# A delta-rule chain that closes its groups two at a time: stages in alternation, the output scale as one GpSimd product, the gates loaded into the product's tile

## The chip, the cores and the metric

The kernel runs on one core of one Trainium2 chip. The metric is the device time of one execution in microseconds (us), start to end; three runs of the kernel before are known. Beside them there is one execution taken by the hardware profiler, with a record for each instruction and each transfer. The five engines are called by their short names in the rows: PE is TensorE (matmuls and transposes), PEld its weight loads, DVE is VectorE, ACT is ScalarE, POOL is GpSimd, and SP is SyncE, which here only issues DMAs. Each engine goes through its own instructions in order.

## The reference

One layer of a bidirectional encoder on 2048 tokens of width 1024. Its branch A is a gated delta rule with 8 heads of width 128, run forward and backward over the sequence and summed; branch B is a long convolution. This is the part that matters:

```
def step(S, xs):
    q_i, k_i, u_i, w_i, attn_i, gl_i = xs
    v_new = u_i - jnp.einsum("nhcd,nhde->nhce", w_i, S)
    o = jnp.einsum("nhcd,nhde->nhce", q_i, S) + jnp.einsum("nhij,nhje->nhie", attn_i, v_new)
    S = S * gl_i[..., None, None] + jnp.einsum("nhcd,nhce->nhde", k_i, v_new)
    return S, o
```

The outputs of both directions are added; per head and token the sum is divided by the root of its mean square, multiplied by a SiLU gate (and by a weight), and projected back to width 1024.

## The kernel before

The stages follow each other: norms, projections, the inner inverses of the delta rule for each chunk, then the chain (method `chain`), then the output projection of branch A (`dn_out`, L1303) and what is left of branch B. The sequence is cut into 16 chunks of 128 tokens for each of the 8 heads, and the chain has 128 steps n; head h = n // 16, step in the head s = n % 16. In step s the forward direction (d = 0) handles chunk s and the backward direction (d = 1) chunk 15 - s, with a state S of 128x128 each. A step is a chain of dependent work between TensorE and the engines that empty its results: `ch <- S, kvq` (L1202), R on VectorE (L1203), `ch <- R, ep` (L1211), Y (L1214 on ScalarE for d = 1, L1216 on VectorE for d = 0), `ch <- Y, kt` (L1223), the new S (L1226) and the outputs o (`po`, L1208 and L1231, emptied at L1238 to L1242). Between them the method yields, and matmuls of an independent projection (`pj`, L635) fill TensorE.

From s = 8 on each step completes two chunks of outputs, since both directions have then been there. Four chunks that lie side by side are a group `o` of 128x4x128, with the sums of squares in `msq` (L1245). After s = 11 and after s = 15 two groups are complete, so there are 16 pairs, 32 groups in all. `finish` closes a group:

- it loads four columns of the norm (`sc <- sqd`, 128x4, 2 KB), and works out the scale with two small operations of VectorE (L1163, L1164) and a power on GpSimd (L1165);
- it loads the gate (`z <- sz`, 128x512, 256 KB);
- it scales o by `sc`, one column for each of four blocks (L1170, four ScalarE activates);
- it transposes the four blocks on TensorE into a PSUM tile (L1174, one buffer) and multiplies them with the gate on VectorE (L1176), then stores the product `og`.

`both` runs `finish` for the first group of a pair and then for the second; the loop over n calls `next(fin)` once at the end of each step, so that a stage of closing goes into a step.

TensorE's instructions keep the order in which the code issues them. The order of the other engines is set ahead of time by a scheduler that sorts instructions by the time at which it expects them to be ready, so that work written for a later step can stand in an earlier place. All loads and stores go through SyncE's one queue (L178 load, L181 store). A tile with k buffers is used in turn: the load of the k-th next one has to wait until the reader of this one is done. Names in the rows: `kvq` and `ep` are the operands of a step (loaded two steps ahead, kvq scaled on GpSimd, L1146), `kt` and `tk` the turned k of the next step (`turn`), `wraw`, `oraw` and `rf` loaded weights and rows which other engines split in two parts (`hh`, `hl`, L206 and L209), `gt`, `th` the gates of branch B.

Of the kernel before, what the change touches and what calls it, by code (L numbers as in the profile page):

```python
# [11 lines left out]
F32 = mybir.dt.float32  # L12
F32R = mybir.dt.float32r
AF = mybir.ActivationFunctionType
ALU = mybir.AluOpType
# [141 lines left out]
class Ring:  # L157
# [6 lines left out]
    def next(self):  # L164
        t = self.t[self.i % len(self.t)]
        self.i += 1
        return t


class K:  # L170
# [949 lines left out]
    def chain(self, P, pp, kvq, ep, sqd, sz_dram, og_dram):  # L1120

        nc = self.nc
        N = H * NCH
        for n in ("eg", "gt", "es"):
            setattr(self, n, P.tile([128, NCH, 16], F32, name=n))
        self.kn = P.tile([128, H, NCH], F32, name="kn")
        nc.gpsimd.memset(self.kn, 0.5)
        nc.gpsimd.tensor_tensor(self.kn, self.ss, self.kn, op=ALU.pow)
        g = self.g
        for d in range(2):  # L1130
            ds_ = slice(8 * d, 8 * d + 8)
            for m, o in ((self.mi[d], self.eg), (self.msr[:, d], self.es), (self.ones, self.gt)):
                ps = pp.tile([128, NCH, 8], F32, name="cs", tag="tr")
                nc.tensor.matmul(ps, lhsT=m, rhs=g[:, :, ds_], start=True, stop=True)
                nc.scalar.activation(o[:, :, ds_], ps, AF.Exp)
        ops, kts = {}, {}
        at = lambda n, d: (n // NCH, n % NCH if d == 0 else NCH - 1 - n % NCH)

        def fetch(n):
            for d in range(2):  # L1140
                h, c = at(n, d)
                a = P.tile([128, 3, 128], F32, name=f"kvq{d}", bufs=3)
                self.load(a, kvq[h][c])
                b = P.tile([128, 2, 128], F32, name=f"ep{d}", bufs=3)
                self.load(b, ep[h][d, c])
                nc.gpsimd.tensor_scalar(a[:, 1], a[:, 1], self.kn[:, h, c:c + 1], None, op0=ALU.mult)  # L1146
                ops[n, d] = (a[:, 0], a[:, 1], a[:, 2], b[:, 0], b[:, 1])

        def turn(n):
            ps = pp.tile([128, 2, 128], F32, name="tk", tag="tr")  # L1150
            for d in range(2):
                nc.tensor.transpose(ps[:, d], ops[n, d][0], self.ident)
            for d in range(2):
                h, c = at(n, d)
                kts[n, d] = P.tile([128, 128], F32, name=f"kt{d}", bufs=2)
                nc.scalar.activation(kts[n, d], ps[:, d], AF.Copy, scale=self.es[:, c, 8 * d + h:8 * d + h + 1])

        def finish(h, g, o, msq):

            cs = slice(4 * g, 4 * g + 4)  # L1160
            sc = P.tile([128, 4], F32, name="sc", bufs=2)
            self.load(sc, sqd[h, 512 * g:512 * g + 512].rearrange("(c p) -> p c", p=128))
            nc.vector.tensor_scalar(sc, sc, EPS, 128.0 * EPS, op0=ALU.add, op1=ALU.mult)  # L1163
            nc.vector.scalar_tensor_tensor(sc, msq, 1.0 / 128.0, sc, op0=ALU.mult, op1=ALU.add)  # L1164
            nc.gpsimd.tensor_tensor(sc, sc, self.mhalf[:, :4], op=ALU.pow)  # L1165
            z = P.tile([128, 512], F32, name="z")
            self.load(z, sz_dram[h, :, 512 * g:512 * g + 512])
            yield
            for j in range(4):
                nc.scalar.activation(o[:, j], o[:, j], AF.Copy, scale=sc[:, j:j + 1])  # L1170
            yield
            ps = pp.tile([128, 4, 128], F32, name="tr", tag="tr")
            for j in range(4):
                nc.tensor.transpose(ps[:, j], o[:, j], self.ident)  # L1174
            og = P.tile([128, 512], F32, name="og")
            nc.vector.tensor_tensor(og, ps.rearrange("p a b -> p (a b)"), z, op=ALU.mult)  # L1176
            self.store(og_dram[h, :, 512 * g:512 * g + 512], og)
            yield

        fin = iter(())  # L1180
        fetch(0)
        fetch(1)
        turn(0)
        for n in range(N):
            h, s = n // NCH, n % NCH
            if s == 0:
                St, O, M = [None, None], {}, {}
            if n + 2 < N:
                fetch(n + 2)
            info = []  # L1190
            for d in range(2):
                c = at(n, d)[1]
                ci = slice(8 * d + h, 8 * d + h + 1)
                k, vr, q, e, p = ops.pop((n, d))
                ps = pp.tile([128, 3, 128], F32, name=f"ch{d}")
                po = pp.tile([128, 2, 128], F32, name="po", bufs=3)
                info.append((c, ci, k, vr, q, e, p, ps, po))
            R, Y = [None, None], [None, None]
            for d, (c, ci, k, vr, q, e, p, ps, po) in enumerate(info):
                R[d] = P.tile([128, 128], F32, name=f"R{d}")  # L1200
                if s:
                    nc.tensor.matmul(ps[:, 0], lhsT=k, rhs=St[d], start=True, stop=True)  # L1202
                    nc.vector.scalar_tensor_tensor(R[d], ps[:, 0], self.eg[:, c, ci], vr, op0=ALU.mult, op1=ALU.subtract)  # L1203
                else:
                    nc.vector.tensor_scalar(R[d], vr, -1.0, None, op0=ALU.mult)
            for d, (c, ci, k, vr, q, e, p, ps, po) in enumerate(info):
                if s:
                    nc.tensor.matmul(po[:, 0], lhsT=q, rhs=St[d], start=True, stop=True)  # L1208
            yield
            for d, (c, ci, k, vr, q, e, p, ps, po) in enumerate(info):  # L1210
                nc.tensor.matmul(ps[:, 1], lhsT=e, rhs=R[d], start=True, stop=True)  # L1211
                Y[d] = P.tile([128, 128], F32, name=f"Y{d}", bufs=2)
                if d:
                    nc.scalar.activation(Y[d], ps[:, 1], AF.Copy, scale=self.an[:, c, ci])  # L1214
                else:
                    nc.vector.tensor_scalar(Y[d], ps[:, 1], self.an[:, c, ci], None, op0=ALU.mult)  # L1216
            if n + 1 < N:
                turn(n + 1)
            yield
            for d, (c, ci, k, vr, q, e, p, ps, po) in enumerate(info):  # L1220
                kt = kts.pop((n, d))
                if s < NCH - 1:
                    nc.tensor.matmul(ps[:, 2], lhsT=kt, rhs=Y[d], start=True, stop=True)  # L1223
                    Sn = P.tile([128, 128], F32, name=f"S{d}", bufs=2)
                    if s:
                        nc.vector.scalar_tensor_tensor(Sn, St[d], self.gt[:, c, ci], ps[:, 2], op0=ALU.mult, op1=ALU.add)  # L1226
                    else:
                        nc.vector.tensor_copy(Sn, ps[:, 2])
                    St[d] = Sn
            for d, (c, ci, k, vr, q, e, p, ps, po) in enumerate(info):  # L1230
                nc.tensor.matmul(po[:, 1], lhsT=p, rhs=Y[d], start=True, stop=True)  # L1231
                g, j = c // 4, c % 4
                if g not in O:
                    O[g] = P.tile([128, 4, 128], F32, name="o", bufs=6)
                    M[g] = P.tile([128, 4], F32, name="msq", bufs=6)
                o = O[g][:, j]
                if s < 8:
                    nc.scalar.activation(o, po[:, 1], AF.Copy)  # L1238
                else:
                    nc.vector.tensor_tensor(o, po[:, 1], o, op=ALU.add)  # L1240
                if s:
                    nc.vector.scalar_tensor_tensor(o, po[:, 0], self.eg[:, c, ci], o, op0=ALU.mult, op1=ALU.add)  # L1242
                if s >= 8:
                    jk = P.tile([128, 128], F32, name="jk")
                    nc.scalar.activation(jk, o, AF.Square, accum_out=M[g][:, j:j + 1])  # L1245
            if s >= 8 and s % 4 == 3:
                for _ in fin:
                    pass

                def both(h, gs, O, M):  # L1250
                    for g in gs:
                        yield from finish(h, g, O[g], M[g])

                fin = both(h, (s // 4, 3 - s // 4), dict(O), dict(M))
            next(fin, None)
            yield
        for _ in fin:
            pass
# [258 lines left out]
```

## Time and profile before

| what | us |
|---|---|
| three runs, median | 3554.59 |
| three runs, lowest and highest | 3553.59, 3556.47 |
| the profiled execution's own time | 3549.07 |
| its span, first to last instruction | 3547.0 |
| TensorE busy in the span | 3319.6 (94%) |
| VectorE, ScalarE, GpSimd busy | 2088.7 (59%), 1489.7 (42%), 1431.3 (40%) |
| the chain, 2288 to 2866 of the span: length, TensorE busy | 578.00, 536.17 |

The profiled execution lies 5.5 us below the median of the runs, and 2.1 us of it lie outside of the span. Sums of rows are to be set against the profiled execution; times of a changed kernel against the runs. In the rows, a number in brackets is the idle time of the engine ahead of the instruction, with the instruction or transfer that ended it.

### The profile page before, as it was taken

The numbers are of one execution on the slowest core, as the hardware profiler recorded it, in microseconds if no ns is written. First come the engines' busy times: TensorE is split into PE (matmuls) and PEld (weight loads), VectorE is DVE, ScalarE is ACT, GpSimd is POOL, SyncE is SP. The second block draws the span as 40 slices with busy tenths as digits, with TensorE's granted clock in tenths as the row PEclk, the third lists the DMA queues.
The fourth block names the chain that finished last, engine by engine and source line by source line (L and its number), as shares of the span: only waits on it lengthen the run. The fifth ranks groups of instructions, "written<-read, shape, count | busy, mean of one in ns | idle before, by whom it ended". The sixth has DMA issues, their size and how long they took to land.

```text
span 3547.0 us, 57648 instructions
## 1 busy us (share of the span) xinstructions
PE 3319.6 (94%) x18370; PEld 2778.6 (78%) x18370; DVE 2088.7 (59%) x4626; ACT 1489.7 (42%) x3744; POOL 1431.3 (40%) x1780
## 2 busy tenths in 40 slices
PE   7999999999998998989889999999999888999999
PEld 6767777888786776777777787888888776888998
DVE  7575455556665568887788734255555558334333
ACT  3334444344554354555554422244444556113221
POOL 3225455677665233223333112433333558124110
PEclk9999999999999999999999999999999999999999
DMA  3343332575454155667766645466776777985442
GB/s 126 134 112 96 103 117 90 172 236 185 140 160 134 58 140 141 160 162 171 177 159 163 158 129 146 138 203 206 211 209 209 228 217 237 300 274 182 145 139 92
DMA packets 734672, 581.59 MB, mean 164 GB/s; under 512 B 252209, under 2 KB 634179, under 8 KB 733346
## 3 DMA queue, kind: packets, MB, share of 16 engines
q1 hardware_dynamic: 734370, 577.92, 56.0%
q8 instruction: 146, 2.39, 0.3%
q14 instruction: 156, 1.28, 0.1%
HBM read 360.45 MB, written 217.25 MB: 163 GB/s over the span
## 4 chain that ended last, share of the span: by engine, by line
PE 57%; DMA 16%; DVE 13%; issue 4%; ACT 4%; POOL 3%; SPq 3%; DVEq 0%; POOLq 0%; ACTq 0%
PE pj L635 29%; PE pj L1303 3%; DMA wraw<-in_wb 2%; PE py L528 2%; PE pf L215 1%; PE pf L213 1%; PE pf L214 1%; SPq L181 1%; DMA kk<-kf 1%; PE ch L1211 1%; SPq L178 1%; DMA e<-cr 1%; DVE xi L1019 1%; DVE tm L1017 1%; PE pj L215 1%
## 5 line engine op out<-in xcount | busy, mean ns | idle before, releaser
L635 PE MATMUL pj<-hh,wh 128*128 128x512 f32 (+1 forms) x2592 | 1042.8, 403 | 28.0 <-DVE wh L208 16.6
L635 PE MATMUL pj<-hl,wh 128*128 128x512 f32 (+1 forms) x2592 | 1033.3, 399 | 3.2 <-POOL hl L209 3.0
L635 PE MATMUL pj<-hh,wl 128*128 128x512 f32 (+1 forms) x2592 | 1031.2, 399 | 1.2 <-POOL wl L209 1.2
L635 PEld LDWEIGHTS pj<-hh,wh 128*128 128x128 f32 x2592 | 495.0, 191 | 131.7 <-DVE wh L208 20.4
L635 PEld LDWEIGHTS pj<-hh,wl 128*128 128x128 f32 x2592 | 493.8, 191 | 93.2 <-issue 4.4
L635 PEld LDWEIGHTS pj<-hl,wh 128*128 128x128 f32 x2592 | 495.1, 191 | 87.7 <-POOL hl L209 3.7
L209 POOL TENSOR_TENSOR wl<-wraw,wh 128x512 fp32r<-128x512 f32 x160 | 216.3, 1352 | 446.4 <-DVE wh L208 347.1
L1146 POOL TENSOR_SCALAR kvq<-kvq,kn 128x128 f32<-128x128 f32 x256 | 153.2, 608 | 291.5 <-DMA kvq<-kvq 51.5
L208 DVE CAST wh<-wraw 128x512 fp32r<-128x512 f32 x160 | 83.9, 524 | 121.3 <-DMA wraw<-in_wb 83.6
L656 DVE SCALAR_TENSOR_TENSOR o<-h_p,chy,o 128x512 f32<-128x512 f32 x96 | 88.1, 925 | 69.2 <-POOL h_p L648 68.1
L213 PE MATMUL pj<-rh,hh 128*128 128x256 f32 x448 | 126.8, 284 | 2.1 <-DVE gt L1365 1.6
L214 PE MATMUL pj<-rl,hh 128*128 128x256 f32 x448 | 126.8, 283 | 0.6 <-POOL rl L209 0.6
L215 PE MATMUL pj<-rh,hl 128*128 128x256 f32 x448 | 126.7, 283 | 0.0
L1366 POOL TENSOR_TENSOR gt<-gt,ex 128x256 f32<-128x256 f32 x64 | 47.9, 749 | 193.3 <-issue 101.1
L953 ACT ACTIVATE e<-e,cum 128x128 f32<-128x128 f32 x256 | 81.8, 390 | 104.4 <-DMA e<-cr 100.5
L984 POOL TENSOR_TENSOR co<-e,beta 128x512 f32<-128x512 f32 x64 | 75.5, 1180 | 123.0 <-DVE beta L980 71.4
L1226 DVE SCALAR_TENSOR_TENSOR S<-S,gt,ch 128x128 f32<-128x128 f32 x224 | 69.1, 345 | 91.8 <-PE ch L1223 91.7
L988 ACT ACTIVATE od<-co 32x128 f32<-32x128 f32 x256 | 78.5, 306 | 95.7 <-DVE co L985 84.5
L655 DVE SCALAR_TENSOR_TENSOR o<-h_p,chy,o 128x512 f32<-128x512 f32 x96 | 92.3, 961 | 43.6 <-ACT o L643 43.5
L209 POOL TENSOR_TENSOR l<-raw,h 128x256 fp32r<-128x256 f32 x128 | 102.0, 813 | 25.5 <-DVE h L208 24.4
L1017 DVE TENSOR_TENSOR tm<-xi 128x30 f32<-128x30 f32 (+14 forms) x240 | 102.1, 425 | 17.0 <-DMA xi<-dg 11.9
L1214 ACT ACTIVATE Y<-ch,beta 128x128 f32<-128x128 f32 x128 | 46.6, 364 | 150.8 <-PE ch L1211 150.0
(348 smaller groups left out, 7771.4 us busy)
## 6 DMA issues: line engine op xcount, KB each, us to landing
kvq<-kvq SPq DMA_DIRECT2D x256, 192.0 KB
wraw<-in_wb SPq DMA_DIRECT2D x160, 256.0 KB
ep<-ep SPq DMA_DIRECT2D x256, 128.0 KB
ru<-ev SPq DMA_DIRECT2D x64, 256.0 KB
rk<-ev SPq DMA_DIRECT2D x64, 256.0 KB
raw<-rk SPq DMA_DIRECT2D x128, 128.0 KB
kf<-ev SPq DMA_DIRECT2D x128, 128.0 KB
kvq<-th SPq DMA_DIRECT2D x64, 256.0 KB
```

The source lines that it names most:

```text
L208: (eng_h or nc.vector).tensor_copy(h, src)
L209: (eng_l or nc.gpsimd).tensor_tensor(l, src, h.bitcast(F32), op=ALU.subtract)
L213: nc.tensor.matmul(ps, lhsT=ah, rhs=bh, start=first, stop=False)
L214: nc.tensor.matmul(ps, lhsT=ah, rhs=bl, start=False, stop=False)
L215: nc.tensor.matmul(ps, lhsT=al, rhs=bh, start=False, stop=last)
L635: self.nc.tensor.matmul(ps, lhsT=a[:, k], rhs=b[k][:, ts_], start=k == 0 and j == 0, stop=k == 7 and j == 2)
L655: nc.vector.scalar_tensor_tensor(out, p[:, 0:512], cw[:, 0:1], out, op0=ALU.mult, op1=ALU.add)
L656: nc.vector.scalar_tensor_tensor(out, p[:, 2:514], cw[:, 2:3], out, op0=ALU.mult, op1=ALU.add)
L953: nc.scalar.activation(e[:, j], e[:, j], AF.Relu, scale=-1.0, bias=self.cum[:, d, h, 4 * g + j:4 * g + j + 1])
L1017: nc.vector.tensor_tensor(tv, x[:, j + 1:, j:j + 1].broadcast_to([128, n, j]), x[:, j:j + 1, :j].broadcast_to([128, n, j]), op=ALU.mult)
L1146: nc.gpsimd.tensor_scalar(a[:, 1], a[:, 1], self.kn[:, h, c:c + 1], None, op0=ALU.mult)
L1303: nc.tensor.matmul(ps, lhsT=w[b][0](x, k), rhs=r[k][y], start=k + n == 0, stop=(k, n) == (7, 2))
```

## The change

Four things change in the closing of groups. (1) The four activates of L1170 become one GpSimd `tensor_tensor` of 128x512 whose second operand is `sc`, repeated along the columns. (2) The gate is loaded into the tile `og` itself, at the start, and the product with the gate is done in place; `z` is gone, `og` has two buffers where it had one, `sc` three where it had two. (3) `finish` yields once more, right after its loads, and `both` goes through the four stages of its two groups in turn. (4) The loop calls `next(fin)` a second time in each step, after `turn`. So a group's stages stand a whole step apart and the two groups half a step; all eight stages are through after four steps.

```
@@ -1158,22 +1158,21 @@
         def finish(h, g, o, msq):
 
             cs = slice(4 * g, 4 * g + 4)
-            sc = P.tile([128, 4], F32, name="sc", bufs=2)
+            sc = P.tile([128, 4], F32, name="sc", bufs=3)
             self.load(sc, sqd[h, 512 * g:512 * g + 512].rearrange("(c p) -> p c", p=128))
+            og = P.tile([128, 512], F32, name="og", bufs=2)
+            self.load(og, sz_dram[h, :, 512 * g:512 * g + 512])
+            yield
             nc.vector.tensor_scalar(sc, sc, EPS, 128.0 * EPS, op0=ALU.add, op1=ALU.mult)
             nc.vector.scalar_tensor_tensor(sc, msq, 1.0 / 128.0, sc, op0=ALU.mult, op1=ALU.add)
             nc.gpsimd.tensor_tensor(sc, sc, self.mhalf[:, :4], op=ALU.pow)
-            z = P.tile([128, 512], F32, name="z")
-            self.load(z, sz_dram[h, :, 512 * g:512 * g + 512])
             yield
-            for j in range(4):
-                nc.scalar.activation(o[:, j], o[:, j], AF.Copy, scale=sc[:, j:j + 1])
+            nc.gpsimd.tensor_tensor(o, o, sc.rearrange("p (a b) -> p a b", b=1).broadcast_to([128, 4, 128]), op=ALU.mult)
             yield
             ps = pp.tile([128, 4, 128], F32, name="tr", tag="tr")
             for j in range(4):
                 nc.tensor.transpose(ps[:, j], o[:, j], self.ident)
-            og = P.tile([128, 512], F32, name="og")
-            nc.vector.tensor_tensor(og, ps.rearrange("p a b -> p (a b)"), z, op=ALU.mult)
+            nc.vector.tensor_tensor(og, ps.rearrange("p a b -> p (a b)"), og, op=ALU.mult)
             self.store(og_dram[h, :, 512 * g:512 * g + 512], og)
             yield
 
@@ -1216,6 +1215,7 @@
             if n + 1 < N:
                 turn(n + 1)
+            next(fin, None)
             yield
@@ -1248,8 +1248,11 @@
                 def both(h, gs, O, M):
-                    for g in gs:
-                        yield from finish(h, g, O[g], M[g])
+                    fs = [finish(h, g, O[g], M[g]) for g in gs]
+                    for _ in range(4):
+                        for f in fs:
+                            next(f)
+                            yield
```

Most lines of the chain move by one in the numbering: L1163 is L1166 in the changed kernel, L1176 is L1175, L1202 and L1203 are L1201 and L1202, L1208 is L1207, L1211 is L1210, L1214 and L1216 are L1213 and L1215; L1223 to L1245 keep their numbers. L1170 is the GpSimd product.

Three places show how the order of instructions moves, all of them in the first two steps (s = 0 and 1) of head 3 (n = 48 and 49; 2497 to 2506 us in the trace of before). On ScalarE, before, the closing of two groups stands as eight activates between the outputs o of one step and the Y of the same step:

```order
1773 L1245 ACTIVATE jk,msq<-o 128x128 x2
1774 L1214 ACTIVATE Y_25624<-ch_25612,beta 128x128
1775 L1156 ACTIVATE kt_25629<-tk,es 128x128
1776 L1156 ACTIVATE kt_25631<-tk,es 128x128
1777 L1238 ACTIVATE o<-po 128x128 x2
1778 L1170 ACTIVATE o<-o,sc 128x128 x8
1779 L1214 ACTIVATE Y_25684<-ch_25668,beta 128x128
```

After, at the same place:

```order
1766 L1245 ACTIVATE jk,msq<-o 128x128 x2
1767 L1213 ACTIVATE Y_25597<-ch_25585,beta 128x128
1768 L1156 ACTIVATE kt_25602<-tk,es 128x128
1769 L1156 ACTIVATE kt_25604<-tk,es 128x128
1770 L1238 ACTIVATE o<-po 128x128 x2
1771 L1213 ACTIVATE Y_25660<-ch_25644,beta 128x128
```

The Y of step 49 now follows the outputs of step 48 directly. On VectorE the same two steps, before, with the two L1163 of the next pair of groups and the product L1176 ahead of R of step 50:

```order
2777 L1203 SCALAR_TENSOR_TENSOR R_25670<-ch_25666,eg,kvq_25525 128x128
2778 L1203 SCALAR_TENSOR_TENSOR R_25673<-ch_25668,eg,kvq_25530 128x128
2779 L1216 TENSOR_SCALAR Y_25681<-ch_25666,beta 128x128
2780 L1226 SCALAR_TENSOR_TENSOR S_25696<-S_25636,gt,ch_25666 128x128
2781 L1226 SCALAR_TENSOR_TENSOR S_25699<-S_25639,gt,ch_25668 128x128
2782 L1163 TENSOR_SCALAR sc<-sc 128x4
2783 L1242 SCALAR_TENSOR_TENSOR o<-po,eg,o 128x128 x2
2784 L1163 TENSOR_SCALAR sc<-sc 128x4
2785 L1176 TENSOR_TENSOR og<-tr,z 128x512
2786 L1203 SCALAR_TENSOR_TENSOR R_25731<-ch_25727,eg,kvq_25600 128x128
```

After:

```order
2780 L1202 SCALAR_TENSOR_TENSOR R_25646<-ch_25642,eg,kvq_25506 128x128
2781 L1202 SCALAR_TENSOR_TENSOR R_25649<-ch_25644,eg,kvq_25511 128x128
2782 L1215 TENSOR_SCALAR Y_25657<-ch_25642,beta 128x128
2783 L1226 SCALAR_TENSOR_TENSOR S_25675<-S_25613,gt,ch_25642 128x128
2784 L1226 SCALAR_TENSOR_TENSOR S_25678<-S_25616,gt,ch_25644 128x128
2785 L1166 TENSOR_SCALAR sc<-sc 128x4
2786 L1242 SCALAR_TENSOR_TENSOR o<-po,eg,o 128x128 x2
2787 L1166 TENSOR_SCALAR sc<-sc 128x4
2788 L1202 SCALAR_TENSOR_TENSOR R_25703<-ch_25699,eg,kvq_25573 128x128
```

The two small operations on `sc` keep their places; the product with the gate no longer stands between them and R (it comes some rows later). SyncE's queue at this place, before:

```order
1797 L178 DMA rf<-og 128x512
1798 L178 DMA kvq_25717<-kvq_85 128x384
1799 L178 DMA kvq_25722<-kvq_85 128x384
1800 L178 DMA sc<-sqd 128x4x1 x2
1801 L178 DMA ep_25719<-ep_93 128x256
1802 L178 DMA ep_25724<-ep_93 128x256
1803 L181 DMA og<-og 128x512
1804 L178 DMA z<-sz 128x512
```

After, from the store of an earlier group on:

```order
1794 L181 DMA og<-og 128x512
1795 L181 DMA gt<-th 128x512
1796 L178 DMA ep_25580<-ep_93 128x256
1797 L178 DMA og<-sz 128x512
1798 L178 DMA rf<-og 128x512
1799 L178 DMA ep_25634<-ep_93 128x256
1800 L178 DMA ep_25639<-ep_93 128x256
1801 L178 DMA kvq_25689<-kvq_85 128x384
1802 L178 DMA kvq_25694<-kvq_85 128x384
1803 L178 DMA sc<-sqd 128x4x1 x2
1804 L178 DMA ep_25691<-ep_93 128x256
```

The load of a gate (`og<-sz`) goes into the tile whose store (`og<-og`) stands three rows ahead of it, and the operands of the next steps and the two `sc` loads are queued behind.

## Rows read from the trace of the kernel before

**Rows 1.** Windows: busy us of each engine in the chain, granted clock, DMA.

```profile
core 0: us, PE busy (x) PEld busy (x) DVE busy (x) ACT busy (x) POOL busy (x), PEclk, DMA share, GB/s
2288.00:2866.00 578.00, 536.17 (x3710) 483.00 (x3709) 320.07 (x1105) 263.82 (x956) 228.66 (x323) 0.99 0.69 205
```

**Rows 2.** Waits of PE, 2288 to 2866: us in total, times, longest.

```profile
PE ch L1223 <- ACT Y L1214: 12.4, 11, 2.5
PE ch L1211 <- DVE R L1203: 6.8, 10, 1.5
PE ch L1202 <- DVE S L1226: 4.8, 5, 1.6
PE po L1208 <- DVE o L1242: 3.7, 4, 1.7
...
PE tr L1174 <- DVE og L1176: 3.3, 1, 3.3
PE tr L1174 <- ACT o L1170: 2.3, 1, 2.3
...
PE pj L1303 <- DVE og L1176: 1.0, 1, 1.0
```

**Rows 3.** Timeline of ACT, step n = 49: start, duration.

```profile
2499.63 2.14 ACT L1170 ACTIVATE o<-o,sc 128x128 f32<-128x128 f32 x7
```

**Rows 4.** Timeline of PE: three of the eight waits behind scalings.

```profile
2359.36 0.49 PE L1208 MATMUL po<-S,kvq 128*128 128x128 f32 x2 [1.18 <-ACT o L1238]
2502.08 0.49 PE L1223 MATMUL ch<-Y,kt 128*128 128x128 f32 x2 [1.93 <-ACT Y L1214]
2763.11 0.49 PE L1223 MATMUL ch<-Y,kt 128*128 128x128 f32 x2 [1.94 <-ACT Y L1214]
```

**Rows 5.** Timeline of POOL and of SP at the same place.

```profile
2498.10 2.02 POOL L1165 TENSOR_TENSOR sc<-sc,mhalf 128x4 f32<-128x4 f32 x2
2500.68 1.53 SPq L178 DMA_DIRECT2D sc<-sqd  x2
```

**Rows 6.** Timeline of DVE at the same place.

```profile
2502.91 0.24 DVE L1163 TENSOR_SCALAR sc<-sc 128x4 f32<-128x4 f32 x1 [2.37 <-DMA sc<-sqd]
...
2504.15 0.17 DVE L1163 TENSOR_SCALAR sc<-sc 128x4 f32<-128x4 f32 x1 [0.56 <-DMA sc<-sqd]
2504.23 0.34 DVE L1242 SCALAR_TENSOR_TENSOR o<-po,eg,o 128x128 f32<-128x128 f32 x1
2504.49 0.68 DVE L1176 TENSOR_TENSOR og<-tr,z 128x512 f32<-128x512 f32 x1
2505.09 0.60 DVE L1203 SCALAR_TENSOR_TENSOR R<-ch,eg,kvq 128x128 f32<-128x128 f32 x2
```

**Rows 7.** Waits of DVE and of SP's queue, 2288 to 2866.

```profile
DVE sc L1163 <- DMA sc<-sqd: 23.1, 18, 2.5
...
SPq L178 <- DMA og<-og: 6.0, 3, 2.7
```

**Rows 8.** Groups by line (L984), and all of L1165: ns min/median/max.

```profile
L984 POOL TENSOR_TENSOR co<-e,beta 128x512 f32<-128x512 f32 x64 | 75.5, 1180 | 123.0 <-DVE beta L980 71.4 <-DMA c<-co 37.7 <-issue 11.1
...
L1165 POOL TENSOR_TENSOR sc<-sc,mhalf x32: 1002/1034/1040, 2336.7 to 2855.2; 128x4 f32<-128x4 f32 x32
```

**Rows 9.** Chain of waits around 2355, and PE's timeline after it.

```profile
2354.84 4.16 DMA og<-og
...
2364.56 0.49 PE L1202 MATMUL ch<-S,kvq 128*128 128x128 f32 x2 [0.72 <-DVE S L1226]
```

**Rows 10.** Chain of waits at the end of the delta-rule chain.

```profile
2854.43 4.85 DMA z<-sz
...
2860.53 3.51 DMA z<-sz
...
2864.16 0.70 DVE og L1176
```

**Rows 11.** All of L1163: ns min/median/max.

```profile
L1163 DVE TENSOR_SCALAR sc<-sc x30: 153/171/1029, 2342.0 to 2843.9; 128x4 f32<-128x4 f32 x30
```

## The prediction

> **What bounds the kernel now.** First the windows of the profile: the change touches only the chain of the gated delta rule, 578 us of the 3547, and there TensorE is busy 536.17 us at a granted clock of 0.99 (the 2.4 GHz level), the other engines at most 55% [rows 1]. So what the edit can win is in the 41.8 us in which TensorE stands still. Then TensorE's waits in that stretch [rows 2]: 12.4 us for Y of ScalarE, 6.8 for R, 4.8 for S, 3.7 for o of VectorE, and at the end of the chain 3.3, 2.3 and 1.0 around the last transposes. What is left of the sum (waits of casts and of loaded weights among them) the change doesn't touch.
>
> Next, the instructions just ahead of each wait. There are two kinds, and both belong to the closing of groups.
>
> The first: a burst of eight scalings on ScalarE. At 2499.63 seven of them run for 2.14 us [rows 3]; the Y of the same step stands behind them in ScalarE's order, and TensorE idles 1.93 us for it [rows 4]. I find eight such waits in the stretch, the first 1.18 us, the last 1.94 [rows 4]. They add up to 9.7 us, of which 7.5 lie in step s=1 of a head and 2.2 in s=12 or 13; the rest of the 12.4 us stands behind casts of loaded weights.
>
> The second follows right after: `sc` has few buffers, so SyncE issues the next two 128x4 loads only when the scaling that reads the old tiles is done, 2500.68 for the first [rows 5]; VectorE holds at L1163 until they land, at 2502.91 and 2504.15, then does the product L1176 (0.68) and only then R at 2505.09 [rows 6]. Over the chain VectorE stands at L1163 for 23.1 us [rows 7]; TensorE feels about 10 of them, most of the waits for R, S and o.
>
> **The change, part by part.** The scaling moves to GpSimd: 128 activates leave ScalarE, 32 products of 128x512 with a broadcast operand come to GpSimd. The same form stands in the profile (L984, 64 times, 1180 ns [rows 8]): 32 x 1.18 = 37.8 us, on an engine that is busy 228.66 of 578 us. Two powers and two products in a row occupy it for 2 x 1.03 + 2 x 1.18 = 4.4 us [rows 8], and kvq's products queue behind. TensorE never waits for kvq in [rows 2], so I cost this at nothing; if that cover were gone, it would cost up to 2.4 us a pair. ScalarE's bursts go away whole: -9.7 us.
>
> Then what is late next. At the place shown, the two powers end at 2500.12 [rows 5], so the products end near 2501.30 and 2502.48. With three `sc` buffers the load of group k still waits for the product of group k-3, and the order shows the two loads after exactly these products. They go out 0.6 us later than today (2500.68 and about 1.2 later), and land by today's distance of 2.2 us at 2503.5 and 2504.8. L1166 keeps its place ahead of the next step's R. The product of the gate is no longer between them (-0.6), so R comes at 2504.8 plus 0.3 for the o between: 2505.1, which is today's 2505.09. TensorE, which would be there 2.1 us sooner, waits those 2.1 us for R. At this place all is given back. Elsewhere a step has a wait without the long load behind it, so I give back 6 of the 7.5 us at s=1 (bounds 0 and 7.5): net -1.5. At s=12 and 13 the products stand a step further from the next loads; of 2.2 I keep 2.0.
>
> The gates go into the tile of the product, `og`, with two buffers. Its load may be issued only when the store of the group two before has landed. A store took 4.16 us [rows 9], and one to five DMAs stand between store and load in the new order, so SyncE, whose one queue carries kvq, ep and `sc` too, holds up to 3 us at each of 30 loads. Today it held three times for such a landing, 6.0 us together [rows 7], and a stop of TensorE of 0.72 us follows one of them [rows 9]. Three holds for 0.72 us would make 30 x 0.24 = 7.2 us; but SyncE already stands waiting for the products at the steps that hurt, so most of it falls into waits that exist. I take +2, bounds 0 and 7.2.
>
> The end of the chain: two gate loads in series, 4.85 and 3.51 us, and the last product begins at 2864.16 [rows 10]. With two tiles both loads can be out early: powers end at 2856.2 (the last starts at 2855.2 [rows 8]), products at 2857.4 and 2858.6, the first transposes' tile is free again near 2859.4; the last gate, loaded after a store of some 4.2 us issued near 2852 and itself 3.5 to 4.9 us long, is there at 2859.7 to 2861.1. The last product ends at 2862.3 to 2863.9 with some slip, instead of 2864.86: -1 to -2.6, I take -1.9.
>
> The extra step between the stages moves only `next(fin)`; on TensorE the transposes of a group stand up to two matmul groups earlier or later, and the PSUM tile they use is free by then ([rows 2] has one such wait, at the end). Nothing.
>
> Sum: -1.5 - 2.0 - 1.9 + 2.0 = -3.4 us. The profiled execution took 3549.07 us, 5.5 less than the median of the three runs (3554.59), with which the new runs are compared: 3554.6 - 3.4 = 3551.
>
> **A rule against the change.** L1163 took 153 ns at least, 171 in the median and at most 1029 [rows 11]: something holds a small operation of VectorE now and then. The Trainium skill, SBUF — State Buffer, section "SBUF: two separate sides", says that VectorE and GpSimd share one pair of ports as an exclusive lock which the one that starts first keeps for its whole instruction; the row's 1029 ns agrees with it, but doesn't show who held the pair. By that rule each new product could hold an operation of VectorE on the path for its whole length; the sum would be that of the fourth rival below. Against it: L1166 can't meet the products that release its own load, because it runs 2 us after them.
>
> **The rivals.** 0.2% of the time, 7.1 us, is about what a measurement here can tell from no change.
>
> (1) The bursts go and nothing comes in their place, chance 0.28. For it: the product L1176 leaves the stretch between the loads and R, and a load that lands sooner than 2.2 us would give all back. Against it: the times at 2499 to 2505. It would give -9.7 - 1.9 = -11.6, and up to 7 more if a part of the 10 us of the second kind goes too: 3543, down to 3536.
>
> (2) Slower, chance 0.13: the landing of stores holds SyncE, and the `sc` loads of each pair come later than the products release them. Each such pair then adds what the hold exceeds, 0.72 us [rows 9] to 1.5. It decides when all 14 pairs of the first seven heads lose more than about 0.9 us over today: 14 x 0.9 = 12.6, less 5.4 of the other terms, makes +7.2; at 1.5 us it is +15.6: 3562 to 3570. For it: 30 loads where three holds stand today. Against: the distance of the loads' consumers, a whole step or more.
>
> (3) The change does not do what it says, that is, moves the wait one for one, chance 0.05 within the forecast's own: only the tail is won and the hold costs 2: 3554.6.
>
> (4) GpSimd holds VectorE, chance 0.04: 14 pairs x 1.18 = 16.5, less 5.4, +11: 3566.
>
> (5) After the chain, from 2866 to 3120 us, DMA is the busy part, and its order shifts by a row or two in the new kernel. No term, but it can move any case by some us either way.
>
> **How the numbers follow.** Forecast 0.55 with (3) (from -9 to +3), (1) 0.28, (2) 0.13, (4) 0.04. Faster by over 7.1 us: most of (1), 0.26, and a tenth of the forecast, 0.06: 0.32. Slower: most of (2) and (4) with some of (5): 0.17. Within: 0.51. The range reaches down to all but the best of (1), 3538, and up to the lower part of (2), 3563; the likeliest case's own is 3545 to 3558.
>
> **What would show it.** In the profile after: no ScalarE instruction at the scaling's line, and Y L1213 no longer 1 to 2 us late at s=1. GpSimd's new product at some 1.18 us. If right, TensorE's wait for R L1210 grows from 6.8 towards 12, with VectorE standing at L1166 for over 25 us in sum. If rival 1 holds, that wait stays at 7 or falls and the stretch ends 10 us sooner. SyncE's wait at L178 for og's own stores grows from 6.0 us to some 40; if its holds appear ahead of a late R or S, it is rival 2. At the end one gate load instead of two in the last chain. The forecast fails if the `sc` loads land much sooner or later relative to R than computed.

## The result: slower by 0.9%

Four runs of the changed kernel have a median of 3586.83 us (3585.88 to 3590.44), four of the kernel before 3555.53 (3553.59 to 3556.81): 1.009 times the time of before, with a 95% interval of 1.0073 to 1.0108, some 31 us. The forecast was 3551, its range ended at 3563. The profiled execution's span is 3584.1 us, 37.1 more than before.

All of the loss lies in the chain. From the first `ch <- R` of step 0 to that of step 127 it takes 601.1 us in the trace after and 562.4 before, 38.7 more; from there to the end the new kernel is about even. These are the starts of `ch <- R` (L1210, before L1211) in the traces, summed over the eight heads by the step s at which they stand, in us; the versions in the lower lines are told below:

```
step s in the head        0-2      3   4-12     13  14-15    chain
before                  117.6   32.1  308.1   47.0   57.5    562.4
after                   142.0   44.7  306.7   43.0   64.8    601.1
e1 gate apart           129.5   46.6  309.4   41.7   65.9    593.1
e6 late second group    143.8   35.3  310.1   43.7   59.6    592.5
e8 32 sc tiles          107.3   46.5  306.1   32.7   66.0    558.5
e9 all three            103.9   39.0  311.2   34.3   59.0    547.4
e10 before + two        109.0   34.7  307.5   37.8   55.4    544.3
e11 holds put back      107.6   35.2  319.7   32.6   58.8    553.9
```

A second trace of a version differs from its first by up to 6 us over the chain (after 605.2, e9 541.7, e10 543.4, e11 549.1), by up to 5 in steps 4 to 12 and by at most 2.2 in the other columns; smaller differences are not read here. The traces of before and after come from the first runs, the others from other chips. The time ahead of the chain is not in the table either: step 0 starts at 2287.5 us after, 2296.0 in e8 and 2302.3 in e9 (2291.7 in its second trace).

So there are two separate losses: 24.4 us in steps 0 to 2, and some 14 us in step 3 and steps 14 and 15 (12.6 + 7.3, less 5.5 at step 4, where transposes stood before). The other steps about cancel: 5 to 12 are 4.1 longer, 13 is 4.0 shorter.

TensorE's waits in the chain of the kernel after (us in total, times, longest), beside [rows 2]:

```profile
PE po L1207 <- DVE o L1242: 16.9, 8, 4.3
PE ch L1201 <- DVE S L1226: 12.3, 5, 4.1
PE tr L1174 <- ACT kt L1156: 12.3, 14, 0.9
PE ch L1210 <- DVE R L1202: 10.7, 6, 4.8
PE ch L1223 <- ACT Y L1213: 5.3, 4, 2.2
```

The wait for ScalarE's Y did fall, 12.4 to 5.3. But o, S and R together grew from 15.3 to 39.9 us, and there is a wait that before does not have at all: transposes that wait for `kt`. The same view for VectorE, SyncE and GpSimd, beside [rows 7]:

```profile
DVE sc L1166 <- DMA sc<-sqd: 27.4, 13, 4.7
DVE og L1175 <- PE tr L1174: 20.7, 15, 3.9
DVE sc L1166 <- POOL kvq L1146: 16.3, 7, 5.5
...
SPq L178 <- DMA og<-og: 45.5, 27, 4.2
...
POOL kvq L1146 <- DMA kvq<-kvq: 94.2, 31, 6.5
```

Of the kernel before, [rows 7] leave out two of these:

```profile
DVE sc L1163 <- POOL kvq L1146: 7.1, 4, 2.8
POOL kvq L1146 <- DMA kvq<-kvq: 51.5, 29, 6.2
```

SyncE's holds for its own stores are what the prediction said (6.0 to 45.5). The two rows of L1166 are one wait: at each of the seven places that the view puts down to GpSimd's kvq product, the load of `sc` landed 0.09 to 0.10 us ahead of L1166, as it did where the view names the load. So VectorE stands there for late loads of `sc` for 43.7 us in sum, in place of 30.2 (23.1 and 7.1) before. The first loss can be followed at the same place as [rows 3 to 6], step 49. This is SyncE's timeline of the kernel after (start, duration), `og<-sz` the load of a gate:

```profile
2504.25 0.32 SPq L178 DMA_DIRECT2D og<-sz  x1
2504.68 0.37 SPq L178 DMA_DIRECT2D kvq<-kvq  x1
...
2513.05 1.37 SPq L178 DMA_DIRECT2D sc<-sqd  x2
```

And this what GpSimd, VectorE and TensorE do there:

```profile
2509.42 0.61 POOL L1146 TENSOR_SCALAR kvq<-kvq,kn 128x128 f32<-128x128 f32 x1 [2.56 <-DVE R L1202]
2509.99 2.02 POOL L1168 TENSOR_TENSOR sc<-sc,mhalf 128x4 f32<-128x4 f32 x2
2511.98 2.04 POOL L1170 TENSOR_TENSOR o<-o,sc 128x512 f32<-128x512 f32 x2
...
2506.49 0.16 DVE L1167 SCALAR_TENSOR_TENSOR sc<-msq,sc 128x4 f32<-128x4 f32 x1
2511.33 0.35 DVE L1226 SCALAR_TENSOR_TENSOR S<-S,gt,ch 128x128 f32<-128x128 f32 x1 [0.79 <-PE ch L1223]
2516.16 0.28 DVE L1166 TENSOR_SCALAR sc<-sc 128x4 f32<-128x4 f32 x1 [4.48 <-DMA sc<-sqd]
2516.36 0.33 DVE L1226 SCALAR_TENSOR_TENSOR S<-S,gt,ch 128x128 f32<-128x128 f32 x1
...
2516.75 0.80 PE L1201 MATMUL ch<-S,kvq 128*128 128x128 f32 x2 [4.10 <-DVE S L1226]
```

Read backwards: TensorE waits 4.10 us for S; S stands on VectorE behind L1166, which waits 4.48 us for a load of 2 KB; that load went out at 2513.05, when the first product on GpSimd was done; the products follow the powers, and the powers began at 2509.99 though the operand L1167 was done at 2506.65. In between GpSimd stood at a kvq product that is ahead of them in its order, until the kvq load issued at 2504.68 was in. (The row names VectorE's R, which ended at 2509.28. The trace has the landing of the load at 2509.24, and the product starts 0.18 us behind it; at the next two loads, 2514.90 and 2515.87, it is 0.19.) That load stands right behind a gate load that SyncE held for 1.1 us until its store had landed, and took 4.6 us itself, against 3.1 in the median of the chain. Six times in the chain, once in each of heads 1 to 6, TensorE stops for 3.3 to 4.8 us behind an L1166 that waits 4.2 to 5.5 us; in the kernel before no stop ahead of the last transposes is longer than 2.5 ([rows 2]).

The second loss, TensorE's timeline at the middle of step 47:

```profile
2503.16 0.63 PE L1174 MATMUL tr<-masks,o 128*128 128x128 f32 x4 [0.85 <-ACT kt L1156]
```

`tk` (the k turned for the next step) and `tr` are the same PSUM tile, with one buffer. The new `next(fin)` issues the transposes right behind `turn`, so they wait until ScalarE has emptied `tk` into `kt`, 14 times by up to 0.9 us, and TensorE's own order keeps all that follows behind them.

### The profile page after: what moved, and what is told of

It is laid out like the page before. It is cut to its first block, busy times and chain, and to the rows that moved or that the text cites. A ratio compares the mean times of both kernels' runs of the same rounds, so it can differ in the third digit from the quotient of the medians.

```text
span 3584.1 us, 57611 instructions
## 1 busy us (share of the span) xinstructions
PE 3333.9 (93%) x18370; PEld 2792.8 (78%) x18370; DVE 2095.8 (58%) x4626; ACT 1456.4 (41%) x3616; POOL 1471.8 (41%) x1812
## 5 line engine op out<-in xcount | busy, mean ns | idle before, releaser
L209 POOL TENSOR_TENSOR wl<-wraw,wh 128x512 fp32r<-128x512 f32 x160 | 216.3, 1352 | 443.5 <-DVE wh L208 343.2
L984 POOL TENSOR_TENSOR co<-e,beta 128x512 f32<-128x512 f32 x64 | 75.2, 1176 | 123.3 <-DVE beta L980 74.6
L1213 ACT ACTIVATE Y<-ch,beta 128x128 f32<-128x128 f32 x128 | 46.9, 366 | 191.4 <-PE ch L1210 188.4
L209 POOL TENSOR_TENSOR l<-raw,h 128x256 fp32r<-128x256 f32 x128 | 103.1, 822 | 24.3 <-DVE h L208 22.6
```

Source lines behind the costliest of these rows:

```text
L209: (eng_l or nc.gpsimd).tensor_tensor(l, src, h.bitcast(F32), op=ALU.subtract)
```

## The experiments

Theory A: the holds of SyncE's queue make kvq and sc late. Theory B: the transposes in the middle of a step wait for the turned k. Theory C, the rival: GpSimd's power and product in a row make sc late by themselves. The runs come in four groups, each on another chip and each with the kernel before beside it: e1 to e4; the mark, e6, e8 and e9; e7 and e10 to e12; and the last three. The kernel before took 3552 to 3578 us there, medians 3562.65 to 3568.65, so the ratios to before are what is compared, and medians only within a group. The expectations give times on the scale of the first runs (before 3555.5, after 3587); a ratio times 3555.5 can be set beside them.

**e1, the gate apart from the product.**

```
-            og = P.tile([128, 512], F32, name="og", bufs=2)
-            self.load(og, sz_dram[h, :, 512 * g:512 * g + 512])
+            z = P.tile([128, 512], F32, name="z", bufs=2)
+            self.load(z, sz_dram[h, :, 512 * g:512 * g + 512])
...
-            nc.vector.tensor_tensor(og, ps.rearrange("p a b -> p (a b)"), og, op=ALU.mult)
+            og = o.rearrange("p a b -> p (a b)")
+            nc.vector.tensor_tensor(og, ps.rearrange("p a b -> p (a b)"), z, op=ALU.mult)
```

> The changed kernel, but the gate is loaded into a tile z of its own (two buffers), and the product is written over the group's own o tile and stored from there: no load has to wait for the landing of a store, all else is as changed. Theory A (the landing of stores holds SyncE's queue; kvq comes late, GpSimd's powers stand behind the late kvq product, sc comes late, VectorE holds ahead of S and R): the excess of the steps s = 1 and 2, 25 us over all heads, goes, 3587 becomes 3560 to 3568, and SyncE's wait for og's own landing (45.5 us) is gone. Theory B (transposes in the middle of a step wait for ScalarE to empty the turned k from the PSUM tile which they share): no change from this, 3587, 14 waits of TensorE for kt remain. Theory C (the power and the product in a row on GpSimd make sc late by themselves): 3583 to 3587, and the waits for S and R stay at 23 us.

Measured: 1.0034 of before (1.0019 to 1.0049), 13 us slower by the medians. The holds are gone, and 12.5 of the 24.4 us of steps 0 to 2; B's part stays.

```profile
SPq L178 <- DMA og<-o: 4.7, 3, 2.6
```

On the expectations' scale this is 3568, the upper end of A's range. But by the steps A is only a half of the first loss, less than expected; VectorE still stands at L1166 for 34 us.

**e2, both stages at the end of a step.** The inserted `next(fin, None)` moves from behind `turn` to the end of the step.

> The changed kernel, but both stages of a step are issued at its end, none in the middle after the k of the next step is turned. Theory B: TensorE's 12.3 us of waits for kt ahead of the transposes go, and with them what follows on VectorE; 3587 becomes 3570 to 3576. Theory A and theory C: the waits for S, R and o (40 us) stay, so no more than B's part can go; if B is wrong and the kt waits only cover others, 3583 to 3587.

Measured: 1.0054 (1.0038 to 1.007), or 3575, within B's range. But the chain in its trace takes 598.5 us against 601.1, and the waits for kt made room for another:

```profile
PE tr L1174 <- DVE og L1175: 12.8, 13, 1.4
```

The two groups' transposes now stand in a row and wait for each other's PSUM tile. So the run does not tell about B; e6 does.

**e3, the scaling back on ScalarE** (the four activates of before in place of the product; the rest as changed).

> The changed kernel, but the scaling is done by the four ScalarE activates of before, all else as changed. Theory C: the sc loads go out earlier, 3587 falls by 10 to 20, to 3567 to 3577. Theory A: sc is late because of the queue and the late kvq, not because of the product; the time stays within 6 of 3587, with ScalarE's bursts ahead of Y back (some 10 us of waits) against 1 to 2 us less in each chain of sc.

Measured: 1.0058 (1.0036 to 1.008), or 3576, at the upper end of C's range; but the interval reaches from there into A's range and overlaps that of the mark below, so the time alone decides nothing. Both things happen: VectorE's waits at L1166 halve (15.2 + 7.0 us against 43.7), so the product has a part in them, as theory C has it, but the bursts are back:

```profile
PE ch L1224 <- ACT Y L1214: 12.1, 8, 2.6
PE po L1208 <- ACT o L1239: 11.4, 4, 3.9
```

**e4, before with the product alone** (L1170 on GpSimd, nothing else).

> The kernel before with nothing changed but the scaling, which is the one GpSimd product. Theory C: slower than before by 10 to 20 us, 3565 to 3575, with VectorE's wait at L1163 above 30 us. Theory A: the product by itself costs and wins little, as the sum of the prediction had it: the bursts' 9.7 us go and most of it comes back as a wait for sc; 3548 to 3558.

Measured: 0.9986 (0.997 to 1.0003), 6 us less by the medians, not told apart from before. The 10 to 20 us of theory C did not come (the chain in e4's trace is longer than before, 569.2 us, but the medians show no loss). The product does what the prediction's first two terms said: the wait for Y falls from 12.4 to 2.7 us and comes back as late sc.

```profile
PE po L1207 <- DVE o L1241: 14.3, 7, 3.4
...
PE ch L1222 <- ACT Y L1213: 2.7, 5, 0.9
...
DVE sc L1163 <- DMA sc<-sqd: 28.6, 16, 4.7
```

**The mark: the changed kernel again.**

> The changed kernel as it is, as the mark for the other three. All theories: slower than before by 0.5 to 0.9%, 18 to 31 us.

Measured: 1.0076 (1.0054 to 1.0098).

**e6, the second group's transposes at the end of the step.**

```
-                    for _ in range(4):
-                        for f in fs:
+                    for i in range(4):
+                        for j, f in enumerate(fs):
+                            if (i, j) == (3, 1):
+                                yield
                             next(f)
```

> The changed kernel, but the last stage of the second group (its transposes) skips the middle of a step and stands at the end of that step; with both stages at the end the transposes had waited for each other's PSUM tile (12.8 us), so this run keeps them a step apart. Theory B: no transposes behind a turned k, TensorE's 12.3 us of waits for kt and VectorE's 20.7 us of waits of the product for its transposes go; 8 to 14 us below the mark. If these waits only cover later ones: within 4 us of the mark.

Measured: 1.0045 (1.0028 to 1.0063), 10.3 us below the mark by the medians, every run of it below every run of the mark. No wait for kt is left, and step 3 falls from 44.7 to 35.3, steps 14 and 15 from 64.8 to 59.6. B holds, at its expected size. Steps 0 to 2 stay (143.8).

**e8, 32 sc tiles.** `name="sc", bufs=3` becomes `bufs=32` (16 bytes a partition each); the scheduler then puts all 32 loads and all 32 L1166 at the start of the chain.

> The changed kernel with 32 sc tiles in place of 3, so that all sc loads are issued at the start of the chain and none waits for a product. Theory A2 (formed from the runs so far: what hurts is VectorE that stands at L1166 in the middle of the chain, whatever makes sc late there, the held queue, the late kvq or the product on GpSimd): VectorE's 46 us of waits at L1166 in the chain go, TensorE's waits for o, S and R fall from 40 us to under 12, and the time is 20 to 30 us below the mark. Theory A as it was (the held queue is what hurts, by late kvq too): SyncE's 45 us of holds stay, kvq comes late at the same steps, and no more than 10 us are won.

Measured: 0.9956 (0.994 to 0.9971), 43 us below the mark and faster than before. SyncE's holds are still there and so is the late kvq (63.6 us), but TensorE hardly waits for what follows from them:

```profile
PE po L1207 <- DVE o L1242: 3.5, 2, 3.0
PE ch L1210 <- DVE R L1202: 3.2, 2, 2.2
PE ch L1201 <- DVE S L1226: 2.9, 2, 2.1
...
SPq L178 <- DMA og<-og: 57.2, 27, 4.5
```

Theory A2 holds, and by more than it gave (20 to 30 us): steps 0 to 2 fall from 142.0 to 107.3, below the 117.6 of before, and step 13, where before lost time too, from 43.0 to 32.7.

**e9, all three mended** (e1, e6 and e8 together).

> The changed kernel with all three mended: gate in its own tile and product over o, the second group's transposes at the end of a step, 32 sc tiles. Theories A2 and B together: none of the three waits is left and ScalarE's bursts are gone, too, so it is faster than the kernel before by 10 to 25 us, 35 to 50 below the mark. If the loss lies in something else (GpSimd's products by themselves, or the interleaving as such), it stays slower than before.

Measured: 0.9915 (0.989 to 0.9941), 31 us faster than before by the medians, 57 below the mark, more than either range of the expectation.

**e7, before with 32 sc tiles.**

> The kernel before with 32 sc tiles in place of 2, nothing else. Theory A2: the waits at L1163 (23 us on VectorE, some 10 on TensorE) go, ScalarE's bursts stay; 8 to 14 us faster than before. If standing at L1163 only covers the bursts: within 4 us.

Measured: 0.9962 (0.9941 to 0.9983), 16 us by the medians, a little more than expected. The late sc was worth that much in the kernel before, too; the bursts stay (`ch` for ScalarE's Y: 13.4 us).

**e10, before with the product and 32 sc tiles.**

> The kernel before with the GpSimd product and 32 sc tiles; gates, order of stages and yields as before. Theory A2: the product's own worth shows when sc can't be late: the bursts' 9.7 us and the 10 of L1163 both go, 15 to 25 us faster than before and 6 to 12 faster than the same with ScalarE. If GpSimd's product costs something by itself (kvq behind it, or the shared port): no faster than the same with ScalarE.

Measured: 0.994 (0.992 to 0.996), 24 us by the medians, 8.6 less than e7, as expected, but the intervals overlap. The traces agree: step 1, where the bursts stood, takes 46.5 us in e7 and 38.9 here. So the product is likely worth something once sc can't take it back.

**e11, e9 with the holds put back** (the gate in the product's tile again).

> As the version with all three mended, but the gate goes into the product's tile again, so that SyncE's holds for landing stores are back (some 45 us); 32 sc tiles and the late second group stay. Theory A2: with sc out of the way the holds cost nothing on TensorE, the time is within 6 us of the version with all three (31 us below before). Theory A as it was: kvq comes late by the holds and costs 10 us or more.

Measured: 0.9945 (0.9925 to 0.9964), by the ratios 10.7 us above e9, which ran on another chip.

**e12, e9 with ScalarE's scaling.**

> As the version with all three mended, but the scaling on ScalarE by four activates. If the product on GpSimd is worth the bursts it removes: 6 to 12 us slower than the version with all three, with TensorE's wait for ScalarE's Y up from 6 to 14 us or more. If the interleaving alone has spread the bursts: within 4 us.

Measured: 0.9978 (0.9966 to 0.9991), some 22 us above e9 by the ratios, more than expected (e9 ran on another chip; e11, beside e12, is 11.6 us faster). The bursts now hold the outputs rather than Y (`po` waits 13.1 us for ScalarE's o).

**e9, e11 and e10 side by side.** Whether the holds cost anything by themselves was open, since e9 and e11 stood in different groups.

> The version with all three mended again, beside the next two. Theory A2: 0.988 to 0.995 of before, and no more than 6 us below the version with the holds. Theory A as it was (holds cost by themselves, through kvq): 10 us or more below it.

> The version with the holds put back and 32 sc tiles, again. Theory A2: within 6 us of the version with all three mended. Theory A as it was: 10 us or more above it.

> The kernel before with the GpSimd product and 32 sc tiles, again. If the interleaving and the second gate tile are worth nothing by themselves: within 4 us of the version with all three mended. If they are worth the end of the chain (some 2 to 4 us) and the spread of the stages: 4 to 12 us above it.

Measured: 0.9908 (0.9891 to 0.9924), 0.9936 (0.9918 to 0.9954) and 0.9912 (0.9895 to 0.9928), medians 3534.63, 3545.32 and 3539.06. The holds cost 10.7 us by the medians, as by the ratios of the first pair, though the intervals still touch; A as it was keeps this much, and A2's 6 us are too few. The traces show where: steps 4 to 12 take 319.7 us in e11 and 311.2 in e9, and 316.1 and 306.5 in the traces of this group. TensorE's longest stop there, 4.70 us (4.65 at the same step in the second trace), stands behind this place on VectorE, in the first trace of e11:

```profile
2664.02 0.43 DVE L208 CAST wh<-wraw 128x512 fp32r<-128x512 f32 x1 [5.03 <-DMA wraw<-in_wb]
2664.36 0.60 DVE L1202 SCALAR_TENSOR_TENSOR R<-ch,eg,kvq 128x128 f32<-128x128 f32 x2
```

It comes from a hold, as SyncE and GpSimd show:

```profile
2654.05 0.32 SPq L178 DMA_DIRECT2D og<-sz  x1
2655.43 0.84 SPq L178 DMA_DIRECT2D kvq<-kvq  x2
...
2661.34 0.33 SPq L178 DMA_DIRECT2D wraw<-in_wb  x1
```

```profile
2659.48 0.60 POOL L1146 TENSOR_SCALAR kvq<-kvq,kn 128x128 f32<-128x128 f32 x1 [3.62 <-PE po L1207]
2660.05 1.26 POOL L209 TENSOR_TENSOR wl<-wraw,wh 128x512 fp32r<-128x512 f32 x1
```

SyncE held the gate load 3.0 us for a store; the kvq load behind it landed at 2659.30, and GpSimd stood at the kvq product (the row names TensorE, whose matmul ended 0.10 us after the landing). The split of the weight, `wl`, stands behind this product, and only when it ended could the next weight go into its one tile `wraw`. It is the same pattern with another tile: an operation off the path, here the cast of a weight whose load came late, stands ahead of R on VectorE. And e10 against e9: 4.4 us apart with intervals that overlap. The alternation of stages and the second gate tile are worth nothing that these runs can show.

## Why the prediction was wrong

**The bursts** (-9.7 us): right. The wait for Y fell by 7.1, to 5.3 us, and no ScalarE instruction is left at the scaling's line.

**The late sc at s = 1** (give back 6 of 7.5, "bounds 0 and 7.5"): this step failed. It took the powers at their old time and added only the products, so the loads went out "0.6 us later". In the trace the first goes out 6.4 us after L1167 (2506.65 to 2513.05), where powers and first product together take 3.1; the other 3.3 are GpSimd at kvq, mostly waiting for the load. The prediction had both parts of it, kvq behind the held queue and work queued on GpSimd, and costed each against its own reader: kvq's reader on TensorE has slack, but the powers that stand behind kvq's product in GpSimd's order have none. Steps 0 to 2 lost 24.4 us in place of a gain of 1.5. What the loads then cost shows in e8, which takes their lateness away: 43 us of time, 34.7 of it in steps 0 to 2. A bound from above that follows a wait along each engine's order would not have stopped at 7.5.

**The holds** (+2, bounds 0 and 7.2): the wait was foreseen, 45.5 us against "some 40"; its price was not. Taking the holds away gave back 12.5 us of steps 0 to 2 (e1), and with sc out of the way 10.7 us of the time (e9 against e11). "Most of it falls into waits that exist" was argued, not read, and wrong.

**The extra step** ("the PSUM tile they use is free by then ... Nothing"): this step failed as well. The tile is shared with the turned k, issued just ahead; 12.3 us of waits, 10.3 us of the time (e6). The orders set side by side with the change are those of ScalarE, VectorE and SyncE; TensorE's is not among them, and [rows 2] can't show a wait that comes only with its new order.

**s = 12 and 13** (-2.0): right in sign, step 13 fell by 4.0, in the mark's trace by 1.8; step 12 did not change by more than 1.3. **The end of the chain** (-1.9): right; from the last `ch <- R` to the first matmul behind the chain it was 13.9 us and is 11.8.

**The clock** was not in the sum. These are windows over the chain, before and after (length, then busy us of TensorE, its weight loads and the other engines, the granted clock third from the end):

```profile
2288.00:2851.00 563.00, 527.77 (x3678) 477.15 (x3677) 315.77 (x1094) 258.98 (x941) 226.65 (x321) 1.00 0.70 208
2287.00:2888.00 601.00, 539.07 (x3673) 488.05 (x3672) 318.54 (x1092) 226.17 (x819) 257.15 (x351) 0.97 0.65 194
```

So of the 38 us more, 26.7 are time in which TensorE stands still (61.9 against 35.2), and for 11.3 it is busy longer with the same matmuls. The latter come from windows such as the third of these, of the kernel after:

```profile
2505.00:2512.70 7.70, 7.65 (x53) 6.84 (x51) 3.18 (x13) 3.94 (x15) 5.05 (x7) 1.00 0.64 186
2512.70:2516.70 4.00, 0.00 (x0) 0.00 (x0) 0.54 (x3) 0.00 (x0) 2.54 (x4) 0.93 0.82 232
2516.70:2523.00 6.30, 6.25 (x24) 5.77 (x25) 2.19 (x8) 0.99 (x3) 1.19 (x2) 0.50 0.31 94
```

After the stop of 4.10 us the granted clock is 0.50, the 1.2 GHz level, for 6.3 us. So this stop cost some 3 us more behind it (an estimate: half of the 6.25 us for which TensorE was busy there).

**The rivals.** Nearest to what came is rival 2, with a chance of 0.13 and a price of 7 to 16 us, in its cause: SyncE's holds make sc late. The way is another one. It had the loads of sc come later than the products release them; at the place followed above the first went out at 2513.05, with its product's end at 2513.02, and the products themselves were late, behind the powers and the kvq product. With it came B, which no rival held, and the clock. Rival 3, a wait moved one for one, is e4: the product alone.

Rival 4 (GpSimd holds VectorE) exists, but not at its price. The rule of the Trainium skill named there (SBUF — State Buffer, section "SBUF: two separate sides"), which the page limits to some forms of VectorE's operations, agrees with these traces. The 1029 ns of L1163 [rows 11] ran beside GpSimd's split of a weight (L209, 2786.19 to 2787.47) and ended 0.02 us behind it. The new product holds one operation of VectorE, the cast of a weight, as in e8:

```profile
2420.93 1.01 DVE L208 CAST wh<-wraw 128x512 fp32r<-128x512 f32 x1 [0.54 <-DMA wraw<-in_wb]
2420.61 2.22 POOL L1170 TENSOR_TENSOR o<-o,sc 128x512 f32<-128x512 f32 x2
```

The first of these products ends at 2421.65 and the cast 0.28 us later, in place of after 0.43 us, its median. In each of the 13 traces with the product one such cast begins beside it and ends 0.28 to 0.29 us behind it, however early it began, and so up to 0.6 us late. That is once in the chain; 38 operations of VectorE begin beside the 32 products in the trace after, none of them L1166 or L1167, and no other than the cast is longer than usual.

What stays open is how the first loss divides between A and C. Without the holds 11.9 us of it stay (e1); the product alone costs steps 0 to 2 5.7 us in the traces (e4, 123.3 against 117.6); the rest was only seen together.

## What to carry to other kernels

When a stage moves to another engine, follow its result through that engine's order and on: what stands ahead of it there, which queue that waits for, which buffer its end releases, and what stands behind the reader of that buffer. A small operation off the path (here 128x4, 170 ns) on an in-order engine can cost more than all the work that was moved, and the cheapest mend was not to speed up its chain but to have its 2 KB loads done long before: 32 tiles of 16 bytes a partition were worth 16 us in the old kernel and 43 in the new one. And look for every tile that shares a buffer by name with the one that a moved step uses: one PSUM tile for two purposes is a wait wherever the two come to stand next to each other.

## What was not expected of the hardware

The product of 128x512 with a broadcast operand on GpSimd took 1048 ns in the mean of 30, less than the 1180 of its nearest row [rows 8]. After each of the five stops of more than 4 us in the chain after, TensorE's first instructions ran at half speed (a 128x512 matmul in 0.63 us in place of 0.39), after the one of 3.33 us they did not; in the kernel before, the one of 2.49 us near 2820 was followed by it too. In the trace of the mark it followed a stop of 2.97 us and not one of 3.11. The length of the stop alone does not tell.
